# An encoder layer on one core: the last block's weight sums moved into its own first stage, dearer DRAM copies in the planner, and a stricter margin for the heads' products

## The chip, the cores and the metric

The kernel runs on one core of a Trainium2 chip. The metric is the device time of one execution in microseconds; of several runs the median is taken. The time before is 2060.51 us, the median of 3 runs (2059.68 to 2060.84).

A core has a matrix engine (TensorE, PE in the profile), a vector engine (VectorE, DVE), a scalar engine (ScalarE, ACT) and two engines that here do little but issue transfers: GpSimd (POOL) and SyncE (SP). Each works through its own list of instructions in order and waits on semaphores for the others. The transfers of POOL and of SP go through two different queues (software and hardware ones) and share 16 DMA engines.

## The reference

One layer over 1024 positions of width 1024, in float32:

```python
h = LN1(alpha * x + 0.5 * SwiGLU_a(x))
h = LN2(alpha * h + HybridMixer(h))
h = LN3(alpha * h + 0.5 * SwiGLU_b(h))

def swiglu(x, w_gate, w_up, w_down):
    return (silu(x @ w_gate) * (x @ w_up)) @ w_down      # inner width 2752
```

The mixer makes one projection of its input into queries, keys and values of 12 heads of 128 channels, 512 Fourier channels and two gates of 1024. The heads come in three groups of four with windows and dilations (128, 1), (512, 4), (2048, 16); each query sees 129 keys of its own dilated neighbourhood, with a relative bias, a softmax and a product with the values. The groups' outputs are mixed by their softmax denominators. The Fourier branch is the real part of a two-dimensional transform. Both branches are projected, gated, added and multiplied with `w_out`.

## The kernel before, in words

**Products.** Each large product is done by a two-level Strassen scheme: 7 products instead of 8 of quarter blocks, whose operands are sums and differences of blocks. A float32 operand is split into a high and a low part, and three products (high by high, high by low, low by high) are added up, so a job on TensorE is a run of twelve matmuls 128x128 by 128x512. The sums of weight blocks that the scheme needs are made in one of two ways: on VectorE after loading the blocks, or in DRAM: SP copies a block to a new place (`tdbt` for block b's down weights, `tdat` for block a's, `vtt` for the values, `wtt` for the output weights), and POOL then issues a transfer that adds another block onto it (line 338, `accum_op`). Of the down weights there are four such sums in three pieces each, so 12 copies (line 822) and 12 accumulations per block.

**Stages, in time of the profiled execution.** Block a's first stage to about 412 us (gate and up products, 21 pairs of column blocks), its down products to 600, a norm and the values to 750, the heads' stage to about 1130 (the Fourier and head pairs are projected, and the attention of heads already projected is done in between), the gates' pairs to 1264, projections and the output product to 1433, block b's first stage to about 1845, its down products to 2054, and the last norm.

**The planner.** One Python class, `Flow`, writes the whole order by hand before anything is compiled. It has a clock for each engine. TensorE's jobs stand in a fixed list. Work of VectorE (`V`), ScalarE (`S`) and POOL (`G`) becomes an instruction when its inputs are reckoned ready, the most urgent first. Loads and DRAM copies (`Q`) are issued in order of when they are needed; each has a size in MB, and the planner reckons its duration as size over a rate of 0.36 MB/us on one DMA line. The heads' products are floats (`F`): they have no place in the list, and are put into TensorE's order before a job as soon as the planner expects them to be ready (`float_ready`, line 244). What the planner reckons sets only the order of each engine's instructions and so of the queues; on the chip each instruction starts when its engine is free and its semaphores allow.

**One step of a head** (names carry group, head and step: `pt002` is group 0, head 0, step 2):

- scores `sc` on TensorE (line 1592),
- bias onto them, into a half page `p`, on VectorE (line 1606), and the row maxima `stat` (`top`, line 1616),
- the exponentials on ScalarE (`exps`, line 1621),
- the turn of `p` on TensorE, into `pt` (line 1637),
- the copy of it into a half page `pT` on ScalarE (`turned`, lines 1644 to 1648),
- where a step has keys of width 192 (half of group 0's last step and all of group 1), two memsets that zero two corners of `pT` on VectorE (`blank`, lines 1651 and 1652),
- the product with the values, `pv`, on TensorE (`values`, lines 1659 and 1664), and its copy out on ScalarE.

Half pages come from a ring of 11. The same ring carries the split of the output weights, `wob` and `wot`: load on SP (line 1829), high part on ScalarE (line 1833), low part on VectorE (line 1837), both stored to DRAM by POOL, after which the half pages are free. This is done in the heads' stage too. Block b's copies and accumulations are tied to the heads' pairs there (`sums_at`, the last line of `ffn`'s call for block b).

Of the kernel before, what the change touches and what calls it, by code (L numbers as in the profile page):

```python
# [74 lines left out]
class Flow:  # L75
# [22 lines left out]
    def V(self, *a, **kw):  # L98
        return self.task("V", *a, **kw)

    def S(self, *a, **kw):
        return self.task("S", *a, **kw)
# [11 lines left out]
    def Q(self, need, mb, fn, deps=(), lead=24.0, **kw):  # L114
        self.loads.append(Node("Q", mb, fn, deps, need, lead, **kw))
        return self.loads[-1]
# [126 lines left out]

    def float_ready(self, force=False):
        for n in list(self.floats):
            if not n.left and self.can(n) and (force or max(n.time(), self.there(n)) <= self.pe + 0.2):
                self.floats.remove(n)
                self.emit(n)

# [33 lines left out]
class Builder:  # L283
# [10 lines left out]
    def half(self, name, dt=F32):  # L294
        return self.sb.tile([P, 512], dt, name=name, tag="s2", bufs=NS2)
# [12 lines left out]
def kernel(  # L308
# [9 lines left out]
    page, half, bank = kb.page, kb.half, kb.bank  # L318
    V, S, G, Q, F, job = fl.V, fl.S, fl.G, fl.Q, fl.F, fl.job
# [27 lines left out]
    W, B, H, J = {}, {}, {}, {}  # L347
# [309 lines left out]
    def ffn(tag, X, w_gu, w_tail, w_dn, load_rest, norm, rest_deps=None, sums_at=None, by_tile=False):  # L657
# [140 lines left out]
        q = Q(J[tl, 0], 0.5, load_tail, pages=1)  # L798
# [11 lines left out]
        blk = {"b11": 0, "b12": 1, "b21": 2, "b22": 3}  # L810
        td = {(n, i): kb.dram([b - a, P, 512], f"td{tag}{n}{i}")
              for n in ("t1", "t2", "t3", "t4") for i, (a, b) in enumerate(PARTS)}
        tdn = {}
# [5 lines left out]
        for si, (to, x0, x1) in enumerate(sums):  # L819
            for i in range(3):  # L820
                def copy(to=to, x0=x0, i=i):
                    nc.sync.dma_start(td[to, i], dn(x0, i) if x0 in blk else td[x0, i])

                def add(to=to, x1=x1, i=i):
                    pool_dma(td[to, i], dn(x1, i), accum_op=OP.add, max_dma_last_dim=4096)
                k = 3 * si + i
                at = sums_at(k) if sums_at else (J[ck[6 + k], 1], J[ck[7 + k], 5])
                a = Q(at[0], 1.0, copy, [tdn[x0, i]] if x0 not in blk else [], lead=0.0)
                tdn[to, i] = Q(at[1], 1.0, add, [a], lead=0.0)


        D_, Y, T, sm = {}, {}, {}, {}
# [57 lines left out]
        for p in (1, 6, 2, 5, 3, 7) if by_tile else (1, 6, 2, 5, 3, 7, 4):  # L890
            for j in range(PAIRS):
                first = p not in (2, 3)
                J[tag, "d", p, j] = n = job((8 if short(p, j) else 12) * MM, step(p, j, SET[p], first), 4 if first and j == 0 else 0, gives=2)
                q = Q(n, 0.5, load_step(p, j), [(HN[PROD[p][0], j], 4.0)] + source_nodes(PROD[p][1], j), 44.0, pages=1)
# [28 lines left out]
        if by_tile:  # L923
# [5 lines left out]
            for i in range((PAIRS + 1) // 2):  # L929
                n = J[tag, "u", 0, 0]  # L930
                deps = [x for j in range(2 * i, min(2 * i + 2, PAIRS)) for x in source_nodes("t4", j)]
                q = Q(n, 0.5, load_b4(i), deps, 88.0 - 8.0 * i, pages=1)
                split(f"qb{tag}{i}", lambda i=i: D_["b", i], lambda t, i=i: D_.__setitem__(("b", i), t), [(q, 1.5)], n,
                      80.0 - 8.0 * i, 512 * min(2, PAIRS - 2 * i), under=(0, 0) if short(4, 2 * i) else None)
            for m in range(4):
                n = J[tag, "u", m, 0]
                q = Q(n, 0.75, load_a4(m), [(HN["a22", j], 4.0) for j in range(PAIRS)], pages=2)
# [310 lines left out]
    vtn = {}  # L1248
    for i, (to, x0, x1) in enumerate((("t1", "b11", "b12"), ("t3", "b12", "b22"), ("t2", "t1", "b22"),
                                      ("t4", "t2", "b21"))):  # L1250
        def copy(to=to, x0=x0):
            nc.sync.dma_start(vt[to], vblk[x0] if x0 in vblk else vt[x0])

        def add(to=to, x1=x1):
            pool_dma(vt[to], vblk[x1], accum_op=OP.add, max_dma_last_dim=4096)
        n = Q(J[("a", 1 + i), 4], 1.0, copy, [vtn[x0]] if x0 in vtn else [], lead=0.0)
        vtn[to] = Q(J[("a", 2 + i), 3], 1.0, add, [n], lead=0.0)

    def value_row(key, g, need):
        def run():  # L1260
# [17 lines left out]
    for p, bk, new in VORDER:  # L1278
        n = PROD[p][1]
        for i in range(2):  # L1280
            value_part(n, i, (vblk if n in vblk else vt)[n][i], [vtn[n]] if n in vtn else (), VJ[p, 0], 14.0)
    for m in range(8):
        st = {}
# [91 lines left out]
    PC = {}  # L1375
# [187 lines left out]
    def attention(idx, g, h, qk, qk_nodes):  # L1563
# [17 lines left out]
        def one(si, step):  # L1581
            n, w = len(step), step[0][2]
            st = {}
# [55 lines left out]
            split_ = w == 192  # L1639

            def turned():
                st["t"] = t = half(f"pT{g}{h}{si}")
                k = 2 * P if split_ else len(cuts) * P
                nc.scalar.activation(t[:, :k], st["tp"][:, :k], AF.Copy)
                if split_:

                    nc.scalar.activation(t[0:64, 3 * P:], st["tp"][0:64, k:k + P], AF.Copy)
                    nc.scalar.activation(t[64:P, k:3 * P], st["tp"][64:P, k:k + P], AF.Copy)

            def blank():  # L1650
                nc.vector.memset(st["t"][0:64, 2 * P:3 * P], 0.0)
                nc.vector.memset(st["t"][64:P, 3 * P:], 0.0)

# [35 lines left out]
            n2 = V(0.63, top, [n1], slack=8.0)  # L1689
            n3 = S(0.63 * n if w > P else 0.5 * n, exps, [n2], slack=8.0)  # L1690
            exp_n[h].append(n3)
            f2 = F(0.11 * len(cuts), turn, [n3], 1, hgives=1)
            n4 = S(0.95 if split_ else 0.54, turned, [f2], frees=1, halves=1, slack=8.0)
            if split_:
                n4 = V(0.25, blank, [n4], slack=8.0)
            f3 = F(0.88 if split_ else 0.22 * len(where), values, [n4], 1, hgives=1, gives=1 if end else 0)
            n5 = S(0.45 if w > P else 1.0, keep, [f3], frees=1, pages=0 if si else 1, slack=8.0)
            done_values.append(n5)
# [86 lines left out]
    SUMS0AT = [(VJ["g", i], VJ["g", i + 1]) for i in range(4)]  # L1785
    wt = {n: kb.dram([2, P, 1024], f"wt{n}") for n in ("t1", "t2", "t3", "t4")}
    wtn = {}
# [3 lines left out]
    for i, (to, x0, x1) in enumerate((("t1", "b11", "b12"), ("t3", "b12", "b22"), ("t2", "t1", "b22"),  # L1791
                                      ("t4", "t2", "b21"))):
        def copy(to=to, x0=x0):
            nc.sync.dma_start(wt[to], out_block(x0))

        def add(to=to, x1=x1):
            pool_dma(wt[to], oblk[x1], accum_op=OP.add, max_dma_last_dim=4096)
        n = Q(SUMS0AT[i][0], 1.0, copy, [wtn[x0]] if x0 in wtn else [], lead=0.0)
        wtn[to] = Q(SUMS0AT[i][1], 1.0, add, [n], lead=0.0)
    for c2 in range(4):  # L1800
        cs = slice(c2 * 256, (c2 + 1) * 256)

# [55 lines left out]
    at = [VJ[p, m] for p in (5, 4, 3) for m in range(4)] + [J[PC[c], p] for c in pairs[:11] for p in PROD]  # L1858
    for r, n in enumerate(("b11", "b21", "b22", "t1", "t3", "t2", "t4")):
        for i in range(2):  # L1860
            k = 4 * r + 2 * i
# [89 lines left out]
    for gi in range(4):  # L1951
        st = {}
# [4 lines left out]
        q = Q(PJ[0], 0.5, load, [(uf_n[gi], 4.0)], 14.0 - gi, pages=1)  # L1957
        t_, s_ = divmod(gi, 2)
        for i in range(2):
# [24 lines left out]
            f = F(0.88, run, [q, (chan_ready, 10.0)], 1, gives=i)  # L1984
            n = S(0.42, hi, [f], pages=1 if s_ == 0 else 0, slack=2.0)
            fold_n.setdefault((t_, i), []).append(V(0.65, lo, [n], frees=1, slack=2.0))

    for i in range(2):
# [4 lines left out]
        q = Q(PJ[0], 0.5, load, (), 22.0 - i, pages=1)  # L1993
# [33 lines left out]
    for t in range(2):  # L2027
        st = {}
# [24 lines left out]
        f = F(3.3, run, fold_n[t, 0] + fold_n[t, 1] + [pos_parts["n", 0], pos_parts["n", 1]], 3, gives=2)  # L2053
        n1 = V(0.3, edges, [f], frees=1, slack=2.0)
        n2 = V(2.2, cosine, [n1], frees=1, pages=2, slack=2.0)
# [24 lines left out]
    f = F(1.7, mid_run, fold_n[0, 0] + fold_n[1, 0] + [pos_parts["n", 0]], 2)  # L2080
# [17 lines left out]
    n = V(0.6, mid_raw, [PJ[2]], pages=2, slack=20.0)  # L2098
# [12 lines left out]
    for c in range(8):  # L2111
        c2, cc = divmod(c, 2)
        st = {}
# [13 lines left out]
        q = gate_load(0, c, PJ[c])  # L2127
# [6 lines left out]
    for c in range(8):  # L2134
        c2, cc = divmod(c, 2)
        st = {}
# [51 lines left out]
        q = gate_load(1, c, FJ[c])  # L2188
        n = S(0.62, sine, [FJ[c]], frees=int(c < 6), halves=1)
        if c > 5:  # L2190
            seeds[c - 6] = [None, n]
        n = V(1.8, outs, [n], frees=2, hgives=1, pages=1)
        n = V(1.23, gate, [n, q], gives=1)
        n = V(1.38, merge, [n] + pj_n[c], gives=2, pages=2 if cc == 0 else 0)
# [82 lines left out]
    def rows2(ck):  # L2277
# [3 lines left out]
        return [[(spilled[2, m], 5.0)] for m in range(8)]  # L2281

    ffn("b", X3, ffn2_gu, ffn2_tail, ffn2_down, lambda m, t: nc.sync.dma_start(t, y2_spill[m]), norm3,
        rows2, lambda k: (J[PC["q", k], 1], J[PC["q", k], 4]), True)
    ln_consts(3, ln3_g, ln3_b, J["b", "d", 3, 8])


# [99 lines left out]
```

## Time and profile before

| What | us |
| --- | --- |
| median of 3 runs | 2060.51 (2059.68 to 2060.84) |
| the profiled execution | 2064.36 |
| its span, from first to last instruction | 2062.6 |
| TensorE busy in the span, 9411 matmuls | 2042.9 |
| VectorE, ScalarE, POOL busy | 1340.1, 890.0, 267.1 |
| mean granted TensorE clock | 0.998 |
| DMA traffic | 442 MB, mean 214 GB/s |

The profile is a page on one execution, and a trace that answers questions. A row of its timelines reads: start in us, duration in us, engine, line of the kernel, operation, output<-inputs, shapes, how many were drawn together, and in square brackets how long the engine stood idle before and what ended that. A row of waits reads: engine, its output and line, <- what it waited for, then the sum in us, how often, and the longest. A row of stretches reads: from:to, length, busy time of TensorE with the number of matmuls, granted clock, share of the DMA engines, GB/s. A group with min/median/max gives durations in ns and the first and last start in us.

### The profile page before, as it was taken

What the parts mean: (1) busy time and instruction counts of PE and PEld (TensorE: products, weight loads), DVE (VectorE), ACT (ScalarE), POOL (GpSimd) and SP (SyncE); (2) the same over time, 40 slices, a digit from 0 to 9 for tenths busy, and PEclk for the clock granted to TensorE, in tenths of its full rate; (3) what the DMA queues carried; (4) which work ended last, traced back from release to release, by engine and by line L of the source; (5) the groups of instructions that cost most, each with busy time, mean ns of one, the idle gap of its engine ahead of it and who ended that gap; (6) DMA issues with size and microseconds to landing.
All of it is one profiled execution on the core that took longest, in us unless ns stands there. A gap on an engine that the chain in (4) does not pass through costs nothing. (4 is left out here: it accounts for less than half of the span.)

```text
span 2062.6 us, 25812 instructions
## 1 busy us (share of the span) xinstructions
PE 2042.9 (99%) x9411; PEld 1701.7 (83%) x9411; DVE 1340.1 (65%) x1930; ACT 890.0 (43%) x1415; POOL 267.1 (13%) x464
## 2 busy tenths in 40 slices
PE   9999999999999999999999999999999999999998
PEld 7888888888888887878888888888888888888886
DVE  7765555576586658555666665687877665575565
ACT  6333333454453324555555443235633333355342
POOL 0122111010001122232122110000011111010000
PEclk9999999999999999999999999999999999999999
DMA  5778875599766568897767668584244433358752
GB/s 204 241 243 251 254 223 163 175 340 403 260 208 184 169 214 267 242 266 222 212 167 222 242 212 343 211 306 168 71 166 175 162 133 125 122 203 287 244 183 94
DMA packets 164143, 442.22 MB, mean 214 GB/s; under 512 B 20370, under 2 KB 42722, under 8 KB 163504
## 3 DMA queue, kind: packets, MB, share of 16 engines
q1 hardware_dynamic: 118928, 288.41, 40.7%
q0 software_dynamic: 45088, 152.16, 24.6%
q8 instruction: 74, 1.21, 0.2%
q14 instruction: 53, 0.43, 0.1%
HBM read 329.63 MB, written 176.91 MB: 246 GB/s over the span
## 5 line engine op out<-in xcount | busy, mean ns | idle before, releaser
L338 POOL DMA_DIRECT2D hsaa<-t2a x21 | 12.0, 569 | 316.6 <-DVE t2a L730 298.5
L1621 ACT ACTIVATE p<-p,stat 128x192 f32<-128x192 f32 (+2 forms) x96 | 42.2, 441 | 24.9 <-DVE stat L1616 23.1
L338 POOL DMA_DIRECT2D n_spill<-y x16 | 9.0, 565 | 298.1 <-DVE y L1061 298.1
L338 POOL DMA_DIRECT2D hsba<-t2b x21 | 11.4, 541 | 271.7 <-DVE t2b L730 229.2
L726 DVE TENSOR_TENSOR t2a<-Da,t2a 128x512 f32<-128x512 f32 x21 | 14.5, 692 | 45.1 <-PE Da L495 45.1
L1606 DVE SCALAR_TENSOR_TENSOR p<-sc,bias 128x512 f32<-128x512 f32 (+1 forms) x40 | 24.7, 621 | 26.2 <-PE sc L1592 20.5
L633 ACT ACTIVATE t2a<-Aa 128x512 f32<-128x512 f32 x21 | 12.6, 600 | 64.9 <-PE Aa L495 64.9
L633 ACT ACTIVATE t2b<-Ab 128x512 f32<-128x512 f32 x21 | 12.6, 600 | 63.8 <-PE Ab L495 63.8
L726 DVE TENSOR_TENSOR t2b<-Db,t2b 128x512 f32<-128x512 f32 x21 | 14.5, 692 | 39.2 <-PE Db L495 39.2
L1411 DVE SCALAR_TENSOR_TENSOR oq<-Dq,b_cols,t2q 128x512 f32<-128x512 f32 x12 | 11.9, 989 | 39.6 <-PE Dq L495 39.6
L1592 PE MATMUL sc<-oq,oq 128*128 128x192 f32 (+2 forms) x192 | 35.4, 330 | 0.0
L1664 PEld LDWEIGHTS pv<-pT,v 128*128 128x128 f32 x240 | 32.2, 191 | 2.2
L718 DVE TENSOR_TENSOR t3a<-Da,t3a 128x512 f32<-128x512 f32 x21 | 14.5, 691 | 29.2 <-PE Da L495 25.1
L1664 PE MATMUL pv<-pT,v 128*128 128x128 f32 x240 | 32.4, 274 | 0.0
L1592 PEld LDWEIGHTS sc<-oq,oq 128*128 128x128 f32 x192 | 30.6, 195 | 2.2
L495 PE MATMUL Db<-Zs40h,usb 128*128 128x512 f32 x84 | 29.4, 391 | 0.1
L495 PE MATMUL Db<-Zs41h,usb 128*128 128x512 f32 x84 | 29.3, 389 | 0.0
L495 PE MATMUL Da<-Xs40h,usa 128*128 128x512 f32 x84 | 29.3, 389 | 0.0
L495 PE MATMUL Da<-Xs41h,usa 128*128 128x512 f32 x84 | 29.3, 389 | 0.0
L1637 PE MATMUL pt<-ident,p 128*128 128x128 f32 x140 | 22.4, 285 | 6.4 <-ACT p L1621 6.3
L718 DVE TENSOR_TENSOR t3b<-Db,t3b 128x512 f32<-128x512 f32 x21 | 14.5, 690 | 21.6 <-PE Db L495 20.0
L1637 PEld LDWEIGHTS pt<-ident,p 128*128 128x128 f32 x140 | 16.9, 144 | 10.5 <-ACT p L1621 8.5
(7481 smaller groups left out, 7306.5 us busy)
## 6 DMA issues: line engine op xcount, KB each, us to landing
qa<-hsas SPq DMA_DIRECT2D x43, 256.0 KB, 5.7
qa<-tdat SPq DMA_DIRECT2D x43, 256.0 KB, 5.4
qb<-hsbs SPq DMA_DIRECT2D x43, 256.0 KB, 4.2
ga<-in_ffn_gu_dram SPq DMA_DIRECT2D x21, 512.0 KB, 6.3
ua<-in_ffn_gu_dram SPq DMA_DIRECT2D x21, 512.0 KB, 7.6
gb<-in_ffn_gu_dram SPq DMA_DIRECT2D x21, 512.0 KB, 3.5
ub<-in_ffn_gu_dram SPq DMA_DIRECT2D x21, 512.0 KB, 4.7
qb<-tdbt SPq DMA_DIRECT2D x33, 256.0 KB, 4.7
```

Of the source, the lines that this page charges most:

```text
L338: nc.gpsimd.dma_start(*a, **kw)
L495: nc.tensor.matmul(out, pick(w, a)[:, k * P:(k + 1) * P], self.cols(xn, b, k), start=first and k == 0 and ti == 0, stop=last and k == 3 an ...
L633: nc.scalar.activation(H[c, t], B[c, "B"], AF.Copy)
L718: nc.vector.tensor_sub(H[c, "t3"], B[c, "D"], H[c, "t3"])
L726: nc.vector.tensor_sub(H[c, "t2"], B.pop((c, "D")), H[c, "t2"])
L1411: stt(views(pages_[i], hf), views(b, None), bias[i], views(H.pop((c, t)), None), op0=OP.add, op1=op)
L1592: nc.tensor.matmul(sv[:, i, :], qk[0][:, qt * P:(qt + 1) * P], qk[1][:, k0:k0 + w], start=True, stop=True, skip_group_check=True)
L1606: stt(p3(), sv, scale, bv, op0=OP.mult, op1=OP.add)
L1621: nc.scalar.activation(p3()[:, i, :], p3()[:, i, :], AF.Exp, bias=stats[h][:, k, 0:1], scale=1.0, accum_out=stats[h][:, k, 1:2])
L1637: nc.tensor.transpose(ps[:, sl * P:(sl + 1) * P], flat[:, x:x + P], ident)
L1664: nc.tensor.matmul(bk[:, at:at + P], env["v"][kc, rows], pt[:, sl * P:(sl + 1) * P], start=not split_ and qt not in seen, stop=last, skip_ ...
```

## The change

There are four parts.

- In `float_ready` a float is put into TensorE's order if it is reckoned ready 0.8 us before the planner's time for TensorE; before, it could be 0.2 us after.
- Copies from DRAM to DRAM count 1.15 MB and accumulations 1.6 MB in the planner, at all three places that make such sums; before, 1.0 each.
- The zeroing `blank` takes the half page `pT` and stands after the maxima; the copy `turned` waits for it. Before, it stood after the copy, and the value product waited for it.
- Block b's sums are tied to its own pairs 6 to 18 (the default that block a uses), and not to the pairs of the heads.

```diff
@@ float_ready
-            if not n.left and self.can(n) and (force or max(n.time(), self.there(n)) <= self.pe + 0.2):
+            if not n.left and self.can(n) and (force or max(n.time(), self.there(n)) <= self.pe - 0.8):
@@ ffn, the sums of the down weights (the same two sizes at vt and wt)
                 at = sums_at(k) if sums_at else (J[ck[6 + k], 1], J[ck[7 + k], 5])
-                a = Q(at[0], 1.0, copy, [tdn[x0, i]] if x0 not in blk else [], lead=0.0)
-                tdn[to, i] = Q(at[1], 1.0, add, [a], lead=0.0)
+                a = Q(at[0], 1.15, copy, [tdn[x0, i]] if x0 not in blk else [], lead=0.0)
+                tdn[to, i] = Q(at[1], 1.6, add, [a], lead=0.0)
@@ one step of a head
             def turned():
-                st["t"] = t = half(f"pT{g}{h}{si}")
+                if not split_:
+                    st["t"] = half(f"pT{g}{h}{si}")
+                t = st["t"]
...
             def blank():
+                st["t"] = half(f"pT{g}{h}{si}")
                 nc.vector.memset(st["t"][0:64, 2 * P:3 * P], 0.0)
...
-            n4 = S(0.95 if split_ else 0.54, turned, [f2], frees=1, halves=1, slack=8.0)
-            if split_:
-                n4 = V(0.25, blank, [n4], slack=8.0)
+            nb = [V(0.35, blank, [n2], slack=8.0, halves=1)] if split_ else []
+            n4 = S(0.95 if split_ else 0.54, turned, [f2] + nb, frees=1, halves=0 if split_ else 1, slack=8.0)
@@ the call for block b
-        rows2, lambda k: (J[PC["q", k], 1], J[PC["q", k], 4]), True)
+        rows2, None, True)
```

The matmuls stay the same in number, and so does the work of VectorE, SP and POOL; ScalarE has two more table loads. Three places show how the order moves.

TensorE at the first head, (0,0). `Aq` and `Dq` are products of the pair in projection, twelve matmuls each, of which the first is shown. Before:

```order
L1592 MATMUL sc000_6753<-oq21_6610,oq20_6609 128x256 x2
L1592 MATMUL sc001_6756<-oq21_6610,oq20_6609 128x256 x2
L495 MATMUL Aq3_6682<-Ya120h_5057,gq3h_6559 128x512
...
L1637 MATMUL pt000_6788<-ident_65,p000_6773 128x128 x4
L1637 MATMUL pt001_6793<-ident_65,p001_6779 128x128 x4
L1592 MATMUL sc002_6798<-oq21_6610,oq20_6609 128x256 x2
L1592 MATMUL sc003_6801<-oq21_6610,oq20_6609 128x192 x2
L495 MATMUL Aq2_6490<-Ys30h_5793,t34q3h_6741 128x512
...
L1664 MATMUL pv000_6843<-pT000_6822,v00_6541 128x128 x4
```

and with the change:

```order
L1592 MATMUL sc000_6752<-oq21_6611,oq20_6610 128x256 x2
L1592 MATMUL sc001_6755<-oq21_6611,oq20_6610 128x256 x2
L495 MATMUL Aq3_6679<-Ya120h_5057,gq3h_6558 128x512
...
L495 MATMUL Aq2_6489<-Ys30h_5793,t34q3h_6742 128x512
...
L1637 MATMUL pt000_6818<-ident_65,p000_6774 128x128 x4
L495 MATMUL Dq3_6823<-Ys10h_5854,t12q3h_6675 128x512
...
L1667 MATMUL pv000_6848<-pT000_6840,v00_6540 128x128 x4
L1637 MATMUL pt001_6853<-ident_65,p001_6776 128x128 x4
```

The turn `pt000` now has two jobs between it and its scores, and `pt001` three.

VectorE at head (1,3), steps 2 and 3. `n10` is a norm row that is loaded back from DRAM and multiplied with its gain, `t12s14l` and `t34s14l` are low parts of the next pair's operands. Before:

```order
L1616 TENSOR_REDUCE stat_8891<-p133_9199 128x2
...
L1651 MEMSET pT132_9238 64x128
L1652 MEMSET pT132_9238 64x128
L1411 SCALAR_TENSOR_TENSOR oq131_9197<-Dq13_9218,b_cols_196,t3q13_9231 128x16x32
L1074 TENSOR_TENSOR n10_9151<-n10_9151,ln1g_9147 128x1024
L363 TENSOR_TENSOR t12s14l_9278<-t12s14_9179,t12s14h_9270 128x1024
L1651 MEMSET pT133_9274 64x128
L1652 MEMSET pT133_9274 64x128
```

and with the change:

```order
L1616 TENSOR_REDUCE stat_8866<-p133_9224 128x2
L1654 MEMSET pT132_9229 64x128
L1655 MEMSET pT132_9229 64x128
L1654 MEMSET pT133_9232 64x128
L1655 MEMSET pT133_9232 64x128
L363 TENSOR_TENSOR t12s14l_9237<-t12s14_9176,t12s14h_9222 128x1024
L1074 TENSOR_TENSOR n10_9184<-n10_9184,ln1g_9125 128x1024
L1077 TENSOR_TENSOR n10_9184<-n10_9184,ln1b_9126 128x1024
L363 TENSOR_TENSOR t34s14l_9281<-t34s14_9213,t34s14h_9254 128x1024
```

The zeroings of both steps have moved ahead of the norm row's gain; the gain now stands ahead of `t34s14l`.

ScalarE at the last head, (2,3). `p230` and `p231` are its two steps, `gs15h` a high part, `os140` and `os141` gates of the pair in projection. Before:

```order
L1621 ACTIVATE p230_9371,stat_8891<-p230_9371,stat_8891 128x128 x4
L1621 ACTIVATE p231_9378,stat_8891<-p231_9378,stat_8891 128x128 x4
L1403 ACT_TABLE_LOAD
L1403 ACTIVATE os140_9410<-As14_9288,b_cols_196 128x512
L358 ACTIVATE gs15h_9414<-gs15_9343 128x1024
L633 ACTIVATE t3s14_9438<-Aq13_9052 128x512
L1644 ACTIVATE pT230_9442<-pt230_9391 128x512
L1644 ACTIVATE pT231_9444<-pt231_9420 128x512
```

and with the change:

```order
L1621 ACTIVATE p230_9343,stat_8866<-p230_9343,stat_8866 128x128 x4
L358 ACTIVATE gs15h_9354<-gs15_9315 128x1024
L1403 ACT_TABLE_LOAD
L1403 ACTIVATE os140_9376<-As14_9239,b_cols_196 128x512
L1621 ACT_TABLE_LOAD
L1621 ACTIVATE p231_9350,stat_8866<-p231_9350,stat_8866 128x128 x4
L633 ACTIVATE t3s14_9403<-Aq13_9016 128x512
L1646 ACTIVATE pT230_9406<-pt230_9385 128x512
L1422 ACT_TABLE_LOAD
L1422 ACTIVATE os141_9377<-t3s14_9403,b_cols_196 128x512
L1646 ACTIVATE pT231_9435<-pt231_9415 128x512
```

Work that needs another table has moved between the exponentials of the two steps, and between the two copies.

More of the change, by code (lines that the diff above doesn't have):

```diff
@@ L1255, in add @@
             pool_dma(vt[to], vblk[x1], accum_op=OP.add, max_dma_last_dim=4096)
-        n = Q(J[("a", 1 + i), 4], 1.0, copy, [vtn[x0]] if x0 in vtn else [], lead=0.0)
-        vtn[to] = Q(J[("a", 2 + i), 3], 1.0, add, [n], lead=0.0)
+        n = Q(J[("a", 1 + i), 4], 1.15, copy, [vtn[x0]] if x0 in vtn else [], lead=0.0)
+        vtn[to] = Q(J[("a", 2 + i), 3], 1.6, add, [n], lead=0.0)
     def value_row(key, g, need):
@@ L1797, in add @@
             pool_dma(wt[to], oblk[x1], accum_op=OP.add, max_dma_last_dim=4096)
-        n = Q(SUMS0AT[i][0], 1.0, copy, [wtn[x0]] if x0 in wtn else [], lead=0.0)
-        wtn[to] = Q(SUMS0AT[i][1], 1.0, add, [n], lead=0.0)
+        n = Q(SUMS0AT[i][0], 1.15, copy, [wtn[x0]] if x0 in wtn else [], lead=0.0)
+        wtn[to] = Q(SUMS0AT[i][1], 1.6, add, [n], lead=0.0)
     for c2 in range(4):
```

## The prediction

> **What bounds the kernel now.** I read the page first, then the stretches of TensorE, then what TensorE waits for, and last the timelines of each engine around each wait.
>
> ```profile
> span 2062.6 us, 25812 instructions
> PE 2042.9 (99%) x9411; PEld 1701.7 (83%) x9411; DVE 1340.1 (65%) x1930; ACT 890.0 (43%) x1415; POOL 267.1 (13%) x464
> ```
>
> TensorE is the bound, so only its own idle time, or time at a lower clock, can be won by a change that leaves its 9411 matmuls as they are. The stretches (length, busy time with matmuls, granted clock, DMA share, GB/s) say where that time lies:
>
> ```profile
> 50.00:410.00 360.00, 360.00 (x1587) 1.00 0.73 220
> 800.00:850.00 50.00, 46.43 (x222) 0.97 0.83 256
> 850.00:900.00 50.00, 49.14 (x252) 1.00 0.90 242
> 900.00:950.00 50.00, 47.22 (x240) 0.97 0.91 276
> 1100.00:1150.00 50.00, 47.97 (x239) 1.00 0.65 204
> 1433.00:1845.00 412.00, 411.95 (x1834) 1.00 0.41 144
> ```
>
> Both FFN first stages are full. The four rows of the heads' stage lack 3.57, 0.86, 2.78 and 2.03 us, 9.24 us together; two of them show a clock of 0.97. TensorE's waits name what it waits for there:
>
> ```profile
> PE pt L1637 <- ACT p L1621: 6.3, 2, 3.6
> PE pv L1659 <- DVE pT L1652: 2.0, 1, 2.0
> PE pv L1659 <- ACT t12q5h L358: 0.8, 1, 0.8
> ```
>
> All are heads' products: two turns of the probabilities (`pt`) wait for the exponentials, two value products (`pv`) for the zeroed halves of `pT`. I call them A (820), D (863), B (905) and C (1107).
>
> **The change, part by part.**
>
> *Sums out of the heads' stage.* Twelve copies on SP's queue and twelve accumulations on POOL's leave this stretch:
>
> ```profile
> L338 POOL DMA_DIRECT2D tdbt<-in_ffn_down_dram x12: 944/982/1004, 805.0 to 1094.8; - x12
> ```
>
> They stand behind A and B. Wait A, on POOL, ScalarE and TensorE:
>
> ```profile
> 804.98 0.94 POOL L338 DMA_DIRECT2D tdbt<-in_ffn_down_dram  x1 [0.49 <-issue]
> 808.70 0.54 POOL L338 DMA_DIRECT2D uf_d<-uf  x1 [1.61 <-DVE uf L1481]
> 821.52 0.63 ACT L609 ACTIVATE usq<-uq 128x512 fp32r<-128x512 f32 x1 [4.79 <-DMA uf_d<-uf]
> 822.16 1.28 ACT L1621 ACT_TABLE_LOAD   x1
> 824.11 2.17 PE L1637 MATMUL pt<-ident,p 128*128 128x128 f32 x8 [3.57 <-ACT p L1621]
> 828.10 0.53 PE L495 MATMUL Aq<-Ys30h,t34q3h 128*128 128x512 f32 x1
> ```
>
> A store issued at 808.70, behind an accumulation, releases ScalarE only at 821.52, 12.8 us later; the first head's exponentials stand behind that instruction. Wait B, on POOL, VectorE and TensorE:
>
> ```profile
> 895.82 0.54 POOL L338 DMA_DIRECT2D wot_d<-wot21l  x1 [1.84 <-DMA tdbt<-in_ffn_down_dram]
> 905.52 0.69 DVE L1837 TENSOR_TENSOR wot41l<-wot41r,wot41h 128x512 fp32r<-128x512 f32 x1 [5.15 <-DMA wot_d<-wot21l]
> 908.28 0.93 PE L1637 MATMUL pt<-ident,p 128*128 128x128 f32 x4 [2.73 <-ACT p L1621]
> 910.15 0.99 PE L495 MATMUL Aq<-Ys30h,t34q6h 128*128 128x512 f32 x1
> 914.31 1.05 PE L1664 MATMUL pv<-pT,v 128*128 128x128 f32 x8
> ```
>
> The same pattern: a POOL store held 1.84 us by the sum, landing some 9.7 us after its issue, holds a half page; VectorE stands 5.15 us, and the bias, maximum and exponentials of the next head come after it.
>
> *The floats' margin.* A product now enters TensorE's line only if the planner expects it ready 0.8 us ahead, not up to 0.2 us late. Jobs between products come twelve matmuls at a time, 12 x 360.00/1587 = 2.72 us, so a float that misses its place enters one job later: in the order, `pt000` has two jobs between it and the scores and not one. An undisturbed first step shows how little room one job gives, on ScalarE and on TensorE:
>
> ```profile
> 988.00 0.50 ACT L1621 ACTIVATE p<-p,stat 128x256 f32<-128x256 f32 x1
> 983.66 1.89 PE L1592 MATMUL sc<-oq,oq 128*128 128x256 f32 x8
> 985.20 0.58 PE L495 MATMUL Aq<-Ya120h,gq9h 128*128 128x512 f32 x1
> 988.12 1.03 PE L1637 MATMUL pt<-ident,p 128*128 128x128 f32 x8
> 988.99 1.19 PE L1592 MATMUL sc<-oq,oq 128*128 128x256 f32 x5
> ```
>
> The turns start at 988.12 while the last of four exponentials still runs to 988.50: no reserve. One job more gives 2.72 us. That covers B's 2.73 almost alone and three quarters of A's 3.57; with the store's landing shortened too, I count A and B as gone. D's 0.80 is under one job as well.
>
> *The zeroing.* Wait C, on VectorE and TensorE:
>
> ```profile
> 1106.24 1.23 DVE L1074 TENSOR_TENSOR n<-n,ln1g 128x1024 f32<-128x1024 f32 x1 [1.88 <-DMA n<-n_spill]
> 1109.11 0.67 PE L1659 MATMUL pv<-pT,v 128*128 128x256 f32 x2 [2.03 <-DVE pT L1652]
> ```
>
> VectorE waits 1.88 us for a norm row's load, then the gain and a split, and only then zeroes `pT`. In the changed order the two zeroings follow the maxima directly, before the gain, so C (2.03) goes. D has a zeroing behind other VectorE work too. In exchange, `turned` on ScalarE now waits for the zeroing; that is long done where its half page is free.
>
> *What the low clock costs.* After A, pt x8 and sc x8 take 828.10 - 824.11 = 3.99 us; the undisturbed ones take (985.20 - 983.66) + (988.99 - 988.12) = 2.41. That is 1.58 lost. After B, half of them take 910.15 - 908.28 = 1.87 against 1.20, and the next job 914.31 - 910.15 = 4.16 against 988.12 - 985.20 = 2.92: 0.67 + 1.24 = 1.91 lost. Together 3.49 us that vanish with A and B.
>
> The Trainium skill ("TensorE: Matmul & The Clock Gate", Part 1, The HAM clock gate) puts the array at half clock after an idle window of about 3.4 us. By that alone only A's loss would be due to idling and B's 1.91 might stay; here the 2.73 us wait is followed by a slow stretch as well, so I go by the row.
>
> *What the new order costs.* At the last head, (2,3), ScalarE's order changes from eight exponentials in a row to four, a split, a table load, an activation, another load, and four more. The rows before:
>
> ```profile
> 1118.27 1.95 PE L1592 MATMUL sc<-oq,oq 128*128 128x128 f32 x16
> 1119.97 0.48 PE L495 MATMUL As<-Ya120h,gs14h 128*128 128x512 f32 x1
> 1124.14 1.28 ACT L1403 ACT_TABLE_LOAD   x1
> 1125.43 0.69 ACT L1403 ACTIVATE os<-As,b_cols 128x512 f32<-128x512 f32 x1
> 1126.02 1.05 ACT L358 ACTIVATE gs15h<-gs 128x1024 fp32r<-128x1024 f32 x1
> 1126.96 0.59 ACT L633 ACTIVATE t3s<-Aq 128x512 f32<-128x512 f32 x1
> 1127.44 1.08 ACT L1644 ACTIVATE pT<-pt 128x512 f32<-128x512 f32 x2
> ```
>
> From scores to the end of eight exponentials 1124.14 - 1118.27 = 5.87; then, start to start, split 0.94, activation 0.59, copy 0.48, half of `pT` 0.54, and two loads at 1.28: 10.98 us until `pT230` is there, 11.30 if each takes its whole busy time. TensorE reaches its value product after scores 1.70, a job 2.92, a job right behind it 2.72, a turn 0.44 and a job 2.92: 10.70. A wait of 0.3 to 0.6; I take 0.5.
>
> The Trainium skill ("ScalarE: Activation LUTs", What ACT_TABLE_LOAD costs) adds a drain of about 1.38 us to each load of 1.28. By it the two extra switches ahead of `pT230` make the wait about 0.5 + 2.76 = 3.3 us. In these rows os starts 0.01 us after the load's end; no drain is seen.
>
> Two other spots have less reserve than before: a zeroing at head (1,0) that needs a half page which a store must free, and n10's gain, now ahead of VectorE work that the last scores need. Neither has a row of its own. Bounds: nothing, if the lighter queues land stores in time, and 5.15 less one job's 2.72, so 2.4, for the first, 1.88 for the second; a gain is excluded, since both only add waits. I take 1.2 for both, nearer to the lower half since the DMA share falls.
>
> *The sums in b's first stage* I cost at nothing. What hides them is shown by a's first stage, 360.00 of 360.00 busy with the same twelve sums in it, at DMA share 0.73; b's has 0.41 now, so it rises to about a's. Their first reader is this, on SP:
>
> ```profile
> L849 SPq DMA_DIRECT2D qb<-tdbt x33: 319/430/978, 1835.7 to 1992.8; - x33
> ```
>
> The last accumulation is set to pair 18 of 21, and pairs take 412/21 = 19.6 us: 1433 + 18.7 x 19.6 = 1800, some 35 us of reserve. If that cover fails, a missed load costs what A did: 3.57 + 1.58 = 5.15. The dearer copies in the planner change no duration; they only move loads.
>
> **Sum.** The profiled execution took 2064.36 us (span 2062.6, 1.76 around it). 2064.36 - 9.24 - 3.49 + 0.5 + 1.2 = 2053.3. The median of the runs shown is 2060.51, 3.85 below the profiled one. If that excess lies outside the waits, the new median is 2049.5; if the excess is the waits themselves being longer under the profiler, it is 2053.3. I take the middle, 2051.4, 9.1 us (0.44%) faster.
>
> **Rivals.**
>
> 1. *A wait comes back at a new place* (chance 0.15). The half pages are a ring, and stores into DRAM free them. For it: D and B both came through this ring. Against: the sums that delayed those stores are gone. One wait like B (2.78 + 1.91 = 4.7) gives 2056.1; one like A, 2056.5; a range of 2055 to 2059.
> 2. *The change does not reach the waits* (0.10). The out blocks' stores and the head loads alone could keep the DMA near 0.9 and A and B half alive, with C gone: the gain is 2.0 + half of (6.35 + 3.49) less 1.7 of new cost, 5.2 on the profile: 2059.2, or 2055.3 if the 3.85 comes off it too.
> 3. *Drains at the table loads* (0.03), by the skill's rule above: ScalarE would stand 2.76 us more ahead of `pT230`, so 2054.2. Against: the 0.01 us in the row.
> 4. *Slower: the sums starve b's first stage* (0.06). SP issues gate and up loads and the copies in one queue; a copy that waits for an accumulation holds the next pair's loads, and TensorE stops for them. Each such stop costs 5.15. It decides from the third on: 2051.4 + 3 x 5.15 = 2066.9; two give 2061.7, no change. For: an accumulation did hold POOL's store 1.84 us at B. Against: block a's 360.00 busy.
>
> **How the numbers follow.** The forecast has 0.66, with its own range 2048 to 2055. About 0.2% (4.1 us) is what a measurement of this kernel tells from no change, so faster means below 2056.4 and slower above 2064.6. Faster: 0.66, the 0.03 of the drains, and half of rivals 1 and a little of 2: 0.77. Same: the rest of 1 and 2 and two stops of 4: 0.16. Slower: 0.07 with what is unforeseen. The range 2047 to 2059 takes in rivals 1 to 3 and leaves out rival 4 and the tails.
>
> **What would show it.** After the change, TensorE's stretches in 800 to 950 should be within 0.3 us of full with clock 1.00, the waits of `pt` for `p` under 1 us together, and `pv` for `pT` L1655 gone; a wait of about half a microsecond should stand at `pv230` near 1120, with ScalarE's loads ahead of it. The stretch of b's first stage should stay full with a DMA share near 0.7. I am wrong if a wait over 2 us stands anywhere in 750 to 1130, if the clock dips there, or if `Ab` or `Db` wait for loads in b's first stage.

## The result and the profile after

The changed kernel takes 2050.15 us, the median of 6 runs (2049.69 to 2050.63), beside 2060.68 for the kernel before on the same chip (6 runs, 2059.68 to 2065.27). The ratio is 0.9945, with a 95% interval of 0.9932 to 0.9957: faster by about 0.55%, inside the range and 1.25 us below the predicted 2051.4.

The head of the page after:

```profile
span 2048.2 us, 25801 instructions
PE 2037.5 (99%) x9411; PEld 1700.3 (83%) x9411; DVE 1339.6 (65%) x1930; ACT 893.6 (44%) x1417; POOL 266.9 (13%) x464
```

The span is 14.4 us shorter; TensorE is busy 5.4 us less with the same 9411 matmuls. TensorE's waits of over half a microsecond (engine, output, what it waited for, sum, times, longest) are two, and the first is the start of the program, which stood there before too:

```profile
PE warm L2293 <- DVE eps L334: 1.4, 1, 1.4
PE pv L1667 <- ACT pT L1646: 0.6, 1, 0.6
```

Its stretches after (length, busy time with matmuls, granted clock, DMA share, GB/s):

```profile
800.00:850.00 50.00, 50.00 (x248) 1.00 0.68 230
850.00:900.00 50.00, 50.00 (x259) 1.00 0.63 207
900.00:950.00 50.00, 50.00 (x271) 1.00 0.49 154
1100.00:1150.00 50.00, 49.44 (x240) 1.00 0.60 200
1420.00:1832.00 412.00, 412.00 (x1835) 1.00 0.63 200
```

The 3.57, 0.86, 2.78 and 2.03 us missing before are gone, and with them the two dips of the clock; what is left is 0.56. The DMA share from 800 to 950 was between 0.83 and 0.91 before and is between 0.49 and 0.68 now. Block b's first stage (the last row) is full at a share of 0.63, where it was 0.41. The sums now stand here, twelve accumulations on POOL, and SP reads the first of them later:

```profile
L849 SPq DMA_DIRECT2D qb<-tdbt x33: 319/424/1158, 1821.3 to 1978.6; - x33
L338 POOL DMA_DIRECT2D tdbt<-in_ffn_down_dram x12: 907/954/1010, 1560.9 to 1773.0; - x12
```

The last is issued 48 us before the first read.

The one new wait is at the last head, on ScalarE and TensorE:

```profile
1107.58 1.04 ACT L358 ACTIVATE gs15h<-gs 128x1024 fp32r<-128x1024 f32 x1
1108.64 1.28 ACT L1403 ACT_TABLE_LOAD   x1
1109.93 0.69 ACT L1403 ACTIVATE os<-As,b_cols 128x512 f32<-128x512 f32 x1
1110.64 1.28 ACT L1621 ACT_TABLE_LOAD   x1
1111.93 0.40 ACT L1621 ACTIVATE p<-p,stat 128x128 f32<-128x128 f32 x1
1113.97 0.57 ACT L1646 ACTIVATE pT<-pt 128x512 f32<-128x512 f32 x1
...
1114.60 1.16 PE L1667 MATMUL pv<-pT,v 128*128 128x128 f32 x8 [0.56 <-ACT pT L1646]
```

Two table loads stand between the halves of the exponentials, and `pT230` ends at 1114.54, just as TensorE's value product is released.

### The profile page after: what moved, and what is told of

It reads as the page before. It is cut to its first block, busy times and chain, and to the rows that moved or that the text cites. A ratio compares the mean times of both kernels' runs of the same rounds, so it can differ in the third digit from the quotient of the medians.

```text
span 2048.2 us, 25801 instructions
## 1 busy us (share of the span) xinstructions
PE 2037.5 (99%) x9411; PEld 1700.3 (83%) x9411; DVE 1339.6 (65%) x1930; ACT 893.6 (44%) x1417; POOL 266.9 (13%) x464
## 4 chain that ended last, share of the span: by engine, by line
PE 98%; DMA 1%; ACT 1%; DVE 0%; issue 0%; SPq 0%; DVEq 0%
PE Ab L495 14%; PE Aa L495 14%; PE Aq L495 8%; PE Db L495 6%; PE Da L495 6%; PE As L495 5%; PE Dq L495 3%; PE Xb L864 3%; PE Xa L864 3%; PE Zb L864 3%; PE Za L864 3%; PE pj L2125 2%; PE v L1291 2%; PE Ds L495 2%; PE wA L2214 2%; PE vB L1230 2%
## 5 line engine op out<-in xcount | busy, mean ns | idle before, releaser
L633 ACT ACTIVATE t2a<-Aa 128x512 f32<-128x512 f32 x21 | 12.5, 598 | 62.5 <-PE Aa L495 62.5
L1411 DVE SCALAR_TENSOR_TENSOR oq<-Dq,b_cols,t3q 128x512 f32<-128x512 f32 x12 | 11.9, 991 | 22.9 <-PE Dq L495 18.8
L1046 ACT ACTIVATE y<-ya,lsa 128x1024 f32<-128x1024 f32 x8 | 9.1, 1143 | 35.7 <-DVE lsa L1041 35.7
```

## The experiments

Two theories stood at the start. One: the sums' transfers slow all other transfers among the heads, and the stricter margin and the early zeroing add the reserve that hides the rest, so that each part does some of it. The other: one of the parts does it all, by the place of the products or by the place of the sums. Four kernels do one part alone, four leave one part out, and four move bytes without moving an instruction of TensorE, VectorE or ScalarE. The three groups ran on three chips. Each ratio is to the kernel before on the same chip: 2064.08 us beside the parts alone (26 runs), 2062.22 beside the parts left out (11), 2062.91 beside the byte kernels (14).

### One part alone

The sums:

```diff
-        rows2, lambda k: (J[PC["q", k], 1], J[PC["q", k], 4]), True)
+        rows2, None, True)
```

> The kernel before with one part alone: block b's sums tied to its own pairs. In TensorE's order the turn pt000 still stands one job behind its scores. Theory (the sums' traffic makes A and B, the margin only adds reserve): A and B shrink to under 1 us each and the clock's 3.49 us go with them, C or its like stays at 2: about 2060.7 - 3.57 - 2.78 - 3.49 + 1.5 = 2052.3, between 2051 and 2055. Rival (one job is too short whatever the DMA does): A and B stay over 2 us each, 2057 or more. The DMA share in 800 to 950 falls from 0.83 to 0.91 to about 0.65 by both.

Measured: 2049.9 us (5 runs, 2049.26 to 2050.19), ratio 0.9933 (0.9908 to 0.9958). That is the whole gain, and more than the theory gave (2051 to 2055). Its stretches, and TensorE's only wait of over 0.2 us:

```profile
800.00:850.00 50.00, 50.00 (x250) 1.00 0.75 250
850.00:900.00 50.00, 50.00 (x258) 1.00 0.55 183
900.00:950.00 50.00, 50.00 (x270) 1.00 0.52 165
1100.00:1150.00 50.00, 50.00 (x243) 1.00 0.61 204
```

```profile
PE warm L2291 <- DVE eps L334: 1.4, 1, 1.4
```

A to D are all gone, with the old margin and the zeroing in its old place. `pt000` is one job behind its scores here and does not wait: one job is enough once the transfers land in time. The stores of the split output weights, from 800 to 915 us, show that they do. The landing times (us, min/median/max) of `wot_d` in the kernel before, then in this one:

```profile
DMA to landing us min/median/max: 2.3/8.5/13.5
```

```profile
DMA to landing us min/median/max: 2.3/3.8/7.9
```

The margin:

```diff
-            if not n.left and self.can(n) and (force or max(n.time(), self.there(n)) <= self.pe + 0.2):
+            if not n.left and self.can(n) and (force or max(n.time(), self.there(n)) <= self.pe - 0.8):
```

> The kernel before with one part alone: floats must be ready 0.8 us ahead. The sums stay among the heads; pt100, pt200, pt010 move to two jobs behind their scores, pt000 stays at one. Theory (the traffic makes the waits, 2.72 us more hides most): B gone, A at pt000 still 3 us or so, C or D perhaps 1: 2060.7 - 2.78 - 1.91 - 2.0 = 2054, between 2052 and 2057. Rival (the margin is the whole change): 2050.5 within 1 us. Second rival (only the sums count): 2058 or more.

Measured: 2056.25 us (10 runs, 2055.18 to 2059.21), ratio 0.9965 (0.995 to 0.998). As the first theory expected: part of the waits go, and A stays. A new wait of 1.1 us stands near 1836, where `Db` waits for `t3b`.

```profile
823.43 1.18 PE L1637 MATMUL pt<-ident,p 128*128 128x128 f32 x4 [3.23 <-ACT p L1621]
```

The early zeroing (`blank` with the half page, before `turned`, as in the change):

```diff
-            n4 = S(0.95 if split_ else 0.54, turned, [f2], frees=1, halves=1, slack=8.0)
-            if split_:
-                n4 = V(0.25, blank, [n4], slack=8.0)
+            nb = [V(0.35, blank, [n2], slack=8.0, halves=1)] if split_ else []
+            n4 = S(0.95 if split_ else 0.54, turned, [f2] + nb, frees=1, halves=0 if split_ else 1, slack=8.0)
```

> The kernel before with one part alone: the zeroing right after the maxima. Theory: C and D go (2.03 and 0.80), A and B stay with their 3.49 of slow clock: about 2058, between 2056.5 and 2059.5. Rival (zeroing early needs its half page early, which the stores hold): new waits of pv for the zeroing, 2060 or more.

Measured: 2068.0 us (10 runs, 2065.59 to 2070.69), ratio 1.0017 (1.0004 to 1.003). A miss: not 2 us faster, rather a little slower. The time is the rival's (2060 or more), but the waits are not those that the rival named. Waits at the old places, one of them longer, and new ones:

```profile
PE pt L1637 <- ACT p L1621: 7.7, 3, 3.9
PE pv L1662 <- ACT pT L1650: 1.6, 1, 1.6
```

The longest, near B, on POOL, ScalarE and TensorE:

```profile
885.59 1.00 POOL L338 DMA_DIRECT2D tdbt<-in_ffn_down_dram  x1
895.01 3.74 POOL L338 DMA_DIRECT2D comb_t<-stat  x5 [8.42 <-issue]
899.33 0.55 POOL L338 DMA_DIRECT2D wot_d<-wot21h  x1
...
906.75 0.60 ACT L633 ACTIVATE t2q<-Aq 128x512 f32<-128x512 f32 x1 [8.51 <-DMA wot_d<-wot21h]
...
909.44 0.97 PE L1637 MATMUL pt<-ident,p 128*128 128x128 f32 x3 [3.92 <-ACT p L1621]
```

POOL stands 8.42 us right behind an accumulation (the kernel before showed 2.01 at the same instruction); the profile names nothing that it waited for. The quarter kernel below names the landing of `stat` at the same instruction; here the store of `stat`, issued at 885.06, took 8.7 us to land, so that is the likeliest. So the store of a half page comes late, and ScalarE waits for its landing. Whether the early zeroing made this worse by holding half pages longer, or the moved order met the transfers at a worse moment, these runs don't tell apart.

The dearer copies (shown at one of three places):

```diff
-                a = Q(at[0], 1.0, copy, [tdn[x0, i]] if x0 not in blk else [], lead=0.0)
-                tdn[to, i] = Q(at[1], 1.0, add, [a], lead=0.0)
+                a = Q(at[0], 1.15, copy, [tdn[x0, i]] if x0 not in blk else [], lead=0.0)
+                tdn[to, i] = Q(at[1], 1.6, add, [a], lead=0.0)
```

> The kernel before with one part alone: copies and accumulations of DRAM reckoned at 1.15 and 1.6. With the sums still among the heads, the planner now sees loads land later, and some value products move one to three jobs back (100 to 103 above all). Theory: A stays since pt000 is still one job behind its scores, B may go: 2055 to 2059. Rival (a planner's number alone gives nothing, since the bytes stay): 2059 to 2062.

Measured: 2062.64 us (10 runs, 2060.66 to 2063.96), ratio 0.999 (0.9978 to 1.0002). No difference that can be measured, as the rival said, though 0.64 us above its range; the theory (2055 to 2059) missed.

### One part left out of the change

The sums back among the heads:

> The changed kernel with the sums put back among the heads (margin, zeroing and dearer costs stay). Theory (traffic makes waits, the margin hides most): 1 to 4 us of waits come back, 2051 to 2055. Rival (the margin and the zeroing are all): 2050.2 within 0.7. Second rival (only the place of the sums counts): 2057 or more.

Measured: 2055.78 us (8 runs, 2052.55 to 2057.26), ratio 0.9966 (0.9956 to 0.9977). That is just above the theory's 2051 to 2055. Without the sums' move the rest of the change gives about the gain of the margin alone. At A the margin does put two jobs between scores and turn here, and a wait is left all the same:

```profile
824.71 1.92 PE L1637 MATMUL pt<-ident,p 128*128 128x128 f32 x8 [1.48 <-ACT p L1621]
```

The other three are the changed kernel with the margin at + 0.2 again, with the zeroing behind the copy again, and with the copies and accumulations at 1.0 again.

> The changed kernel with the floats' margin put back to 0.2 us late. Turns stand one job (3.1 to 3.2 us) behind their scores almost everywhere. Theory: the lighter DMA leaves few late instructions, but there is no reserve, so small waits of 0.2 to 1 us at several heads: 2051 to 2054. Rival (reserve is not needed once the sums are gone): 2050.2 within 0.7. Second rival (the margin is the whole change): 2057 or more.

Measured: 2049.92 us (4 runs, 2049.57 to 2050.17).

> The changed kernel with the zeroing back behind the copy. Its value products of width 192 stand one job (2.9 to 3.1) or two behind the turn. Theory: C was one late load on VectorE, and such come back at one or two places of 1 to 2 us: 2050.5 to 2053. Rival (the margin alone gives the zeroing its room): 2050.2 within 0.5.

Measured: 2049.66 us (4 runs, 2049.53 to 2050.83).

> The changed kernel with copies and accumulations reckoned at 1.0 again. TensorE's order in the heads' stage is the same as with the change. Theory: same time, 2050.2 within 0.7. Rival (block a's and b's first stages need the dearer costs to keep their loads in time): 2052 or more, with waits for gate or up loads.

Measured: 2049.97 us (4 runs, 2049.85 to 2050.12).

All three have the ratio 0.9944 (0.9927 to 0.9961), the same as the whole change. Neither margin, zeroing nor prices add anything once the sums are away. For the margin and the zeroing the theory had expected small waits to come back; none did: every stretch of 50 us from 750 to 1150 is full in both kernels. These two also lack the 0.56 us wait at the last head, which is too small to show in the medians.

### Bytes without instructions

The sums' move also changes the planner's order for the heads. To keep the order, the kernel before got the real sums in block b's first stage, and among the heads the same copies and accumulations at the same places, onto a scratch tensor that nobody reads, with a size that can be set. The orders of TensorE, VectorE and ScalarE are those of the kernel before, row for row; those of SP and POOL too, up to block b's first stage.

```diff
+        if sums_at:
+            tx = {(n, i): kb.dram([b - a, P, 512], f"tx{tag}{n}{i}")
+                  for n in ("t1", "t2", "t3", "t4") for i, (a, b) in enumerate(PARTS)}
...
+                    def copy(to=to, x0=x0, i=i):
+                        nc.sync.dma_start(tx[to, i][:min(CB, PARTS[i][1] - PARTS[i][0])], (dn(x0, i) if x0 in blk else tx[x0, i])[:min(CB, PARTS[i][1] - PARTS[i][0])])
+
+                    def add(to=to, x1=x1, i=i):
+                        pool_dma(tx[to, i][:min(AB, PARTS[i][1] - PARTS[i][0])], dn(x1, i)[:min(AB, PARTS[i][1] - PARTS[i][0])], accum_op=OP.add, max_dma_last_dim=4096)
+                    at = sums_at(3 * si + i)
+                    a = Q(at[0], 1.0, copy, [txn[x0, i]] if x0 not in blk else [], lead=0.0)
+                    txn[to, i] = Q(at[1], 1.0, add, [a], lead=0.0)
...
-                at = sums_at(k) if sums_at else (J[ck[6 + k], 1], J[ck[7 + k], 5])
-                a = Q(at[0], 1.0, copy, [tdn[x0, i]] if x0 not in blk else [], lead=0.0)
-                tdn[to, i] = Q(at[1], 1.0, add, [a], lead=0.0)
+                a = Q(J[ck[6 + k], 1], 1.0, copy, [tdn[x0, i]] if x0 not in blk else [], lead=0.0)
+                tdn[to, i] = Q(J[ck[7 + k], 5], 1.0, add, [a], lead=0.0)
```

`CB` and `AB` are the blocks of 128x512 that a copy and an accumulation move: 1 each (called the quarter kernel), then 1 and all (3 or 4), all and 1, all and all.

> The order of TensorE, VectorE and ScalarE is that of the kernel before, row for row, and so is that of SP and POOL up to block b's first stage. The sums among the heads write to a scratch place and move one block of 128x512 where they moved 3 or 4 (a quarter to a third of the bytes); the real sums are made again in block b's first stage, as in the changed kernel. Theory (bytes): with the same order the waits A to C fall below 2 us together, 2050 to 2053. Rival (the place in the queues and the waits of POOL for SP's copies count, not the bytes): 2057 or more. Second rival (VectorE's and ScalarE's order, which moving the sums also changed): 2057 or more, and it stays so in all four kernels of this form.

Measured: 2050.79 us (4 runs, 2050.33 to 2050.97), ratio 0.9941 (0.9924 to 0.9958).

> As the quarter kernel, but with accumulations of full size; the copies are cut to a quarter. Theory (the accumulations stand in the queue of POOL's own stores, which hold the half pages): nearly as slow as before, 2056 to 2062. Rival (bytes wherever they go): about half way, 2053 to 2057, and the same for the copies alone.

Measured: 2053.18 us (4 runs, 2053.09 to 2055.68), ratio 0.9953 (0.9936 to 0.9969).

> As the quarter kernel, but with copies of full size; the accumulations are cut to a quarter. Theory (POOL's queue): 2050 to 2053, the copies go through SP's queue and hold no store. Rival (bytes wherever they go): 2053 to 2057, as with the accumulations alone.

Measured: 2054.56 us (5 runs, 2053.28 to 2055.17), ratio 0.9956 (0.9942 to 0.997).

> As the quarter kernel, but copies and accumulations of full size: the sums are made twice, among the heads on a scratch place and in block b's first stage. By all theories of the heads' stage as slow as before, 2059 to 2066. Were the sums in block b's first stage not free, it would be slower than before by 1 us or more at the same waits, and a wait of Ab or Db for loads would stand there.

Measured: 2061.85 us (10 runs, 2057.68 to 2066.0), ratio 0.9991 (0.9979 to 1.0004).

The stretch from 800 to 910 us of the kernel before and then, each in a fence of its own, of the sums alone moved, a quarter of the bytes, full accumulations, full copies and both full (length, busy time of TensorE, its weight loads, VectorE, ScalarE, POOL, granted clock, DMA share, GB/s):

```profile
800.00:910.00 110.00, 102.79 (x503) 85.49 (x503) 65.91 (x109) 60.58 (x137) 31.10 (x53) 0.98 0.88 264
```

```profile
800.00:910.00 110.00, 110.00 (x570) 94.31 (x569) 74.02 (x124) 68.01 (x158) 28.17 (x51) 1.00 0.62 206
```

```profile
800.00:910.00 110.00, 109.68 (x555) 92.29 (x555) 71.03 (x120) 65.15 (x153) 32.36 (x55) 1.00 0.72 225
```

```profile
800.00:910.00 110.00, 107.50 (x532) 90.15 (x531) 68.16 (x115) 63.31 (x144) 31.84 (x55) 0.98 0.83 244
```

```profile
800.00:910.00 110.00, 107.76 (x534) 90.32 (x533) 69.13 (x119) 62.87 (x144) 32.30 (x55) 0.98 0.78 248
```

```profile
800.00:910.00 110.00, 102.93 (x494) 85.26 (x493) 60.79 (x99) 57.54 (x130) 30.64 (x52) 0.97 0.83 250
```

So the bytes do it: one order, four sizes, and TensorE's missing time there goes 0.32, 2.50, 2.24, 7.07 us. My first guess, that the accumulations do it since they share POOL's queue with the stores, falls: the copies on SP's queue cost no less (2054.56 against 2053.18). The stores themselves bear this out. Those of `wot_d` on POOL's queue, from 800 to 915, take 5.8 us to land in the quarter kernel (median), 6.6 with full accumulations, 6.5 with full copies, and 8.5 with both, which is what they took before. For the copies it is bytes and not packets: SP's queue sends 119312 packets with quarter copies and with full ones, and 8.4 MB more with the full ones. The place of the instructions, and the changed order of the other engines, fall as rivals too, since the quarter kernel keeps both and takes 2050.79.

The last kernel also prices the sums in block b's first stage: it makes them there on top of those among the heads, and is not slower than before.

C is explained by the same. In the quarter kernel VectorE's order at head (1,3) is the old one, gain before split before zeroing. The load of the norm row in the kernel before, and in the quarter kernel (KB, us to landing), and VectorE there:

```profile
n<-n_spill SPq DMA_DIRECT2D x1, 512.0 KB, 12.5
```

```profile
n<-n_spill SPq DMA_DIRECT2D x1, 512.0 KB, 5.4
```

```profile
1093.50 1.23 DVE L1088 TENSOR_TENSOR n<-n,ln1g 128x1024 f32<-128x1024 f32 x1
1094.64 1.23 DVE L364 TENSOR_TENSOR t12s14l<-t12s,t12s14h 128x1024 fp32r<-128x1024 f32 x1
1095.83 0.17 DVE L1665 MEMSET pT<- 64x128 f32 x1
```

The row's load takes 7.1 us less, the gain starts without a wait, and the zeroing behind it is in time.

## Why the prediction was right, and where not

**What bounds it.** Right: TensorE's four waits and two slow stretches among the heads were what could be won, and all of it was won, less the new 0.56.

**Sums out of the heads' stage.** Right in kind and too small in size. I named the sums as what stands behind A and B, and gave the margin and the zeroing a share of the work. Moved alone, the sums give 2049.9, everything. Their effect is not the two places where a wait names an accumulation, but that stores and loads among the heads land later, also those that no accumulation holds.

**The floats' margin.** The step "one job more covers B almost alone and three quarters of A" did not carry the result. Alone the margin gives 0.35%, and left out of the change it costs nothing. In the kernel with the margin alone the planner still leaves `pt000` one job behind its scores, and A at 3.23. With two jobs there, as with everything but the sums' move, A is 1.48: in one execution each, about 1.8 us less where 2.72 were reckoned.

**The zeroing.** That it ends C is right, but C needed no ending of its own. In the kernel with the early zeroing alone, VectorE zeroes first and stands still for the norm row afterwards, and no value product waits for a zeroing:

```profile
1100.22 0.17 DVE L1655 MEMSET pT<- 64x128 f32 x1
1104.94 1.23 DVE L1074 TENSOR_TENSOR n<-n,ln1g 128x1024 f32<-128x1024 f32 x1 [4.55 <-DMA n<-n_spill]
```

What the prediction left out is why the row was late: before, its load took 12.5 us, and with the bytes gone it is in time, and C is gone in the old order too. Alone, the early zeroing brought no gain (ratio 1.0017), since other waits grew. D was counted among the waits for a zeroing; its row names `t12q5h`, a split on ScalarE, and ScalarE had stood there for a store:

```profile
861.63 0.63 ACT L1833 ACTIVATE wot11h<-wot11r 128x512 fp32r<-128x512 f32 x1 [3.96 <-DMA wot_d<-wot11h]
```

**The low clock.** 3.49 us counted as gone with A and B: the granted clock is 1.00 in every stretch. The size was right as well: each dip is 3.41 us at a clock of 0.50 (rows in the last section), so two cost 3.41. That B's 1.91 came of its own wait, as I took it, is borne out there: shorter waits are followed by such a dip too.

**The last head.** I took 0.5; it is 0.56. The rival of the drains, 3.3, is out: the gate's activation starts at 1109.93, 0.01 after the load's end (1108.64 + 1.28), and the next load at 1110.64, 0.02 after that activation's end.

**Two other spots**, 1.2 us: nothing is there: beside the program's start and the last head, TensorE's waits are of some 0.2 us at most, and none stands at either spot.

**Block b's first stage at nothing.** Right: 412.00 of 412.00 busy, at a share of 0.63 where I said about 0.7. Rival 4 did not come.

**The sum.** On the profiled execution I had 2053.3; it took 2049.92. Of the 3.4 us between, 1.2 are the two spots. The heads of the two pages say where the other 2.2 lie: TensorE is busy 5.4 us less and idle 9.0 us less (14.4 less 5.4). The idle time was reckoned nearly right, 9.24 less the new 0.5. Of busy time the sum had only the dips, 3.49, so 1.9 us more went than it holds; they lie in small steps, which I can't name singly. Against that stands the choice at the end: I took half of the 3.85 us by which the profiled execution lay over the median. The profile after lies 0.23 us below its median (2049.92 against 2050.15). That fits the second of the two readings, longer waits in that execution, by which alone I would have said 2053.3; it isn't shown, since only one execution of the kernel before has a trace. A sum 3.4 us too slow and a choice 2.2 us too fast nearly cancel. That the forecast came within 1.25 is in part luck; the mechanism doesn't rest on it.

**The scatter** says the same. On one chip, six runs each, the kernel before took from 2059.68 to 2065.27 and the changed one from 2049.69 to 2050.63. That the waits' chance part is what went is the likeliest reading, and was not shown run by run.

**Rival 2**, that the stores and loads alone would keep the DMA near 0.9, is refuted by the share of 0.49 to 0.68. Rival 1 is refuted at once by the list of waits.

No kernel here beats the change by more than the measurement tells: the sums' move alone (2049.9) and the change without the zeroing (2049.66) stand within its scatter. Of the four edits one is needed.

## What to carry to other kernels

When several engines wait at different places for stores, reloads and half pages, look for one load on the DMA behind all of them before giving each wait a cause of its own: here moving 24 transfers whose results the products did not read for another 700 us ended four waits, whose rows named three different things. In this kernel the background copies belong into the stage whose DMA share is low (0.41), with time left before their first reader (48 us), and not into the one that is at 0.9. To tell bytes from order, keep the instructions where they are and cut the sizes.

## What the hardware showed that I had not expected

The cost of the bytes is not a sum. Over the quarter kernel (2050.79), full accumulations cost 2.4 us and full copies 3.8, together 6.2; both at once cost 11.1. With both the runs scatter widely (2057.68 to 2066.0); by the fastest run of each kernel it is 2.8, 3.0 and 7.4. The profiled executions, each the slowest of its kernel, show 2.50 and 2.24 us missing and one dip of the clock each for one kind, and 7.07 with three dips (from 824.14, 871.93 and 912.89) for both. One explanation, which was only argued, is that a lateness under the reserve of one job is free and what goes beyond counts in full, with a dip of the clock on top.

The clock dips after shorter waits than those seen before the change. TensorE's wait in the kernel with full accumulations, then in the one with full copies:

```profile
822.25 1.92 PE L1651 MATMUL pt<-ident,p 128*128 128x128 f32 x8 [1.65 <-ACT p L1635]
```

```profile
902.40 1.18 PE L1651 MATMUL pt<-ident,p 128*128 128x128 f32 x4 [2.02 <-ACT p L1635]
```

In these traces a dip in the heads' stage is 3.41 us at a clock of 0.50 (one, in the kernel with the early zeroing alone, is twice as long). Where an execution has several, they begin whole multiples of 3.413 us apart: before the change at 823.96 and 909.29, which is 25 times. On this grid, here are the 3.41 us with the wait and the 3.41 us behind them, for full accumulations, for full copies, and for C before the change:

```profile
820.79:824.20 3.41, 1.79 (x9) 1.00 0.68 192
824.20:827.61 3.41, 3.41 (x10) 0.50 0.02 5
```

```profile
899.10:902.51 3.41, 1.39 (x7) 1.00 1.05 344
902.52:905.93 3.41, 3.41 (x10) 0.50 0.96 296
```

```profile
1107.27:1110.68 3.41, 1.57 (x9) 1.00 0.01 3
1110.68:1114.09 3.41, 3.41 (x16) 1.00 0.74 250
```

Waits of 1.65 and 2.02 us are followed by half the clock, while C's 2.03 before the change was followed by none. The Trainium skill ("TensorE: Matmul & The Clock Gate", Part 1, The HAM clock gate) names an idle window of about 3.4 us; these rows don't agree that so long a wait is needed. The length of the wait alone doesn't decide, since its place on the grid sets how much work the 3.41 us still hold: 1.39 us with full copies and 1.57 at C. Nor does the busy time alone: the 1.79 us with full accumulations, 1.75 of them turns, are followed by a dip, and 1.78 us in the kernel with the early zeroing alone (from 860.90) are not. Whether turns count for less stays open.
